# Four bias tables in place of one: replicating a relative-bias table head by head, with pauses, in a two-layer hybrid encoder

## Chip, cores and metric

The kernel runs on 1 core of one Trainium2 chip. The metric is the device time of one execution in microseconds (us), as the median of the runs of one kernel.

## What is computed

The reference is an encoder of two layers on 2048 tokens of width 1024, all in float32. Each layer normalises x, multiplies it by one wide input matrix (1024 x 3584), splits the result among four mixers of 256 channels, gates and joins their outputs and multiplies by an output matrix. The change lies in what mixer D (2-D neighbourhood attention, four heads of 64) needs: a bias that is looked up from a small learned table of each head by the relative row and column of query and key.

```python
def hybrid_layer(x, norm_g, w_in, w_out, ..., na_rpb):
    h = rmsnorm(x, norm_g)
    proj = jnp.einsum("bsd,de->bse", h, w_in)      # split into groups A, B, C, D
    ...
    y_d = neighborhood_attn(d_q, d_k, d_v, na_rpb) * jax.nn.silu(d_z)
    y = jnp.concatenate([y_a, y_b, y_c, y_d], axis=-1)
    return x + jnp.einsum("bse,ed->bsd", y, w_out)

def neighborhood_attn(q, k, v, rpb):               # rpb (4 heads, 15, 31)
    ...
    bias = jnp.take(rpb[:, dr], dc, axis=-1)       # dr, dc: relative row and column
    scores = jnp.where(col_ok[:, None, :], scores + bias[None], NEG_INF)
    p = jax.nn.softmax(...)
```

## The kernel before

**Staging.** Channels stand on the 128 partitions and tokens in four chunks of 512 columns; two chunks at a time are resident (slots s0 and s1). Every float32 operand of the large products is split into a high and a low part, and each product is three matmuls (line 906). A weight tile is loaded in two halves of 256 KB into one of three buffers `wraw` (`load_w`, line 879), split by ScalarE into `whi` (line 218) and by VectorE into `wlo` (line 219), and then used by 12 matmuls of 512 columns for each chunk (`run`, line 894). The matmul helper `mm` is line 135, and VectorE's instructions all stand at line 128.

**Order of the work.** The order is written by generators in Python. After each group of 8 of the large matmuls `run` calls `point()` (line 180), which advances every generator of the lists `evs`, `units` and `bg` by one step; `hold(n)` (line 212) lets n such points pass. There are 864 groups in the kernel: 336 for the input product of a layer, 96 for its output product. In the first half of a layer the first three weight tiles are run for one chunk and then again for the other (3 points a tile, so weights are loaded twice as densely there), and the tiles between are run for both chunks (6 points a tile).

Attention is cut into *units* (line 646): one kind (C or D), chunk, head pair and quarter. A unit begins at most every 5 points (`SPACING`), loads q, holds 7 points and then issues its score matmuls at the next one. A group of four units begins once its `ready` mark and its bias table are `done` (`add_units`, line 785): units of chunk 0 of layer 0 need the table of layer 0, and all others the table of layer 1. The marks come from the tiles of the input product: `("qd", 0, 0)` 8 points after the eighth tile and `("qd", 0, 1)` 8 points after the twelfth tile of the second half. The output product of a chunk needs the attention outputs Y of that chunk, loaded and split by `place_y_steps` (line 343).

On top of this a scheduler of the framework puts each engine's instructions in the order in which they become ready in its own timeline, by priority, so that a transfer without a dependency can be issued long before its place in the program. `tc.keep_in_program_order` pins an instruction behind the one that was traced before it on the same engine. All transfers of the kernel are issued by SyncE (SP), one after the other: a transfer that waits holds up those behind it.

**The bias table.** `bias_steps(l)` (line 792) runs once for each layer: for layer 0 as a background generator as soon as chunk 1 is staged (`early`, line 1126), for layer 1 as a unit after the last units of chunk 0 (line 1078). It copies the 18 KB of the layer's four zero-padded head tables to 128 rows of `rep` in DRAM (line 795, 2256 KB), holds 4 points, and gathers for each head 128 shifted windows of 737 elements into `bm` (line 804, 368.5 KB each; the first three in the `ks` buffers, the last in a `vt` buffer of the attention). Then nine mask pieces `bmk` are loaded (line 809), GpSimd subtracts (line 817) and the result is stored to `bias` (line 821); each of the nine takes 6 points of the program.

Of the kernel before, what the change touches and what calls it, by code (L numbers as in the profile page):

```python
# [18 lines left out]
P = 128  # L19
# [11 lines left out]
RPW = 47  # L31
RPR = 24
# [3 lines left out]
def window(i, j):  # L36
    R, C = DROWS[i][1], DCOLS[j][1]
    return (15, 5, C) if (R, C) == (16, 24) else (R, 4, C)
# [33 lines left out]
def trunk(ctx, tc, xT, w_in, w_out, par, sink, rpb, fg, trig, cmask, dmask, out):  # L72
    nc = tc.nc
    pe, act, dve, pool, sp = nc.tensor, nc.scalar, nc.vector, nc.gpsimd, nc.sync
# [14 lines left out]
    def T(pool_, shape, dt, tag, bufs, name=None):  # L89
        uid[0] += 1  # L90
        return pool_.tile(shape, dt, tag=tag, bufs=bufs, name=f"{name or tag}_{uid[0]}")
# [54 lines left out]
    def dram(name, shape, dt=F32):  # L146
        return dr.tile(shape, dt, name=name)

    LP = []
    for l in range(DEPTH):  # L150
        L = {"par": par_t[l]}
        L["aw"] = L["par"][:, PAW:PAW + 62]
        L["bw"] = L["par"][:, PBW:PBW + 6]
        for nm, w in (("lbh", 2), ("lbq", 2), ("sink", 4), ("nsink", 4)):
            L[nm] = const.tile([P, w], F32, name=f"{nm}{l}")
        L["KD"] = [dram(f"KD{l}_{p}", [2, P, SEQ]) for p in range(2)]
        L["QD"] = [dram(f"QD{l}_{p}", [2, 64, SEQ // P, 2 * P]) for p in range(2)]
        L["KC"] = [dram(f"KC{l}", [2, P, SEQ])]
        L["QC"] = [dram(f"QC{l}_{p}", [2, 64, SEQ // P, 2 * P]) for p in range(2)]
        L["VC"] = dram(f"VC{l}", [P, 2, SEQ // P, P])  # L160
        L["VD"] = [dram(f"VD{l}_{p}", [64, 32, 2 * P]) for p in range(2)]
        L["G"] = [dram(f"G{l}_{e}", [P, SEQ]) for e in range(8)]
        L["Y"] = [dram(f"Y{l}_{e}", [P, 2, SEQ]) for e in range(4)]
        L["X"] = dram(f"X{l}", [DM, SEQ])
        L["rep"] = dram(f"rep{l}", [P, 4 * RPR * RPW])
        L["bias"] = dram(f"bias{l}", [4, P, MTOT])
        LP.append(L)

# [43 lines left out]
    def hold(n):  # L212
        for _ in range(n):
            yield
# [576 lines left out]

    def bias_steps(l):
        L = LP[l]
        W = 4 * RPR * RPW
        tc.keep_in_program_order(sp.dma_start(out=L["rep"], in_=rpb[l:l + 1, :].broadcast_to([P, W])))
        yield from hold(4)
        n = 15 * RPW + 32
        Ms = []
        for h in range(4):
            M = T(ap_, [P, 2 * CH], F32, "ks", KSB, "bm") if h < 3 else T(ap_, [P, 2 * CH], F32, "vt", VTB, "bm")  # L800
            base = L["rep"][0:1, :]
            src = bass.AP(tensor=base.tensor, offset=base.offset + h * RPR * RPW + 7 * RPW + 15,
                          ap=[[16 * W - RPW, 8], [W - 1, 16], [1, n]])
            sp.dma_start(out=M[:, :n], in_=src)
            Ms.append(M[:, :16 * RPW].rearrange("p (r c) -> p r c", c=RPW))
        for (o, sz, i, j) in MOFF.values():
            R, rr, C = window(i, j)
            mk = T(ap_, [P, CH], F32, "pth", PTB, "bmk")
            sp.dma_start(out=mk[:, :sz], in_=dmask[:, o:o + sz])
            r0, c0 = ROW_M0[i], COL_M0[j]  # L810
            mkv = mk[:, :sz].rearrange("p (g r c) -> p g r c", r=rr, c=C)
            yield
            yield
            for p in range(2):
                t = T(ap_, [P, 2, CH], F32, "prob", PRB, "bmo")
                for hh in range(2):
                    pool.tensor_tensor(out=t[:, hh, :sz].rearrange("p (g r c) -> p g r c", r=rr, c=C), in0=mkv,
                                       in1=Ms[2 * p + hh][:, r0:r0 + R, c0:c0 + C].rearrange(
                                           "p (r g) c -> p g r c", r=rr), op=ALU.subtract)
                yield from hold(2)  # L820
                sp.dma_start(out=L["bias"][2 * p:2 * p + 2, :, o:o + sz].rearrange("h q n -> q h n"), in_=t[:, :, :sz])
        done.add(("bias", l))
# [251 lines left out]
    for l in range(DEPTH):  # L1074
        add_units(l, "d", 0, ("qd", l, 0))
        add_units(l, "c", 0, ("qc", l, 0))
        if l == 0:
            waiting.append((lambda: all(("c", 0, 0, 1, j) in done for j in range(4)), deque([lambda: bias_steps(1)])))
        for c in (1, 2, 3):
            add_units(l, "d", c, ("qd", l, 1))  # L1080
            add_units(l, "c", c, ("qc", l, 1))
# [44 lines left out]
    def early():  # L1126
        while (0, 1) not in acts:
            yield
        yield from bias_steps(0)
# [80 lines left out]
```

## Time and profile before

| | |
|---|---|
| median of 3 runs | 2021.67 us (2020.09 to 2022.21) |
| the profiled execution's own time | 2031.42 us |
| its span, first to last instruction | 2029.4 us |
| mean granted TensorE clock | 0.988 of full speed |
| TensorE matmul busy | 1953.2 us (96%), 9600 instructions |
| VectorE busy | 1484.6 us (73%) |
| ScalarE busy | 1042.1 us (51%) |
| GpSimd busy | 147.3 us (7%) |
| DMA | 402.74 MB, mean 198 GB/s |

Times of rows are microseconds from the start of the span unless marked ns. Engines: PE is TensorE (PEld its weight loads), DVE VectorE, ACT ScalarE, POOL GpSimd, SP SyncE; SPq is a transfer's issue on SyncE's queue. Names such as `wraw<-in_w_in_dram` are output and input tiles of an instruction, with buffer numbers left out.

### The profile page before, as it was taken

The page shows a single profiled execution, that of the slowest core. Times are in us where ns is not written, and L with a number is a line of the kernel's source. Part 1 is how long each engine was busy: PE and PEld are TensorE (multiplying, and loading weights), DVE is VectorE, ACT ScalarE, POOL GpSimd, SP SyncE. Part 2 cuts the span into 40 slices and gives each one's busy share as a digit, 9 for nine tenths or more (in the row PEclk, how much of TensorE's full clock was granted, in tenths as well). Part 3 has the DMA queues.
Part 4 walks back from the last instruction along what each step waited for, and adds up shares of the span by engine and source line. Part 5 has one row for each costly group of instructions (what it writes and reads, how often), then busy time and mean ns, then how long its engine had stood idle before and what let it go on. Part 6 is the DMA issues. An engine that isn't in the chain of part 4 may idle for free.

```text
span 2029.4 us, 29478 instructions
## 1 busy us (share of the span) xinstructions
PE 1953.2 (96%) x9600; PEld 1637.2 (81%) x9600; DVE 1484.6 (73%) x3209; ACT 1042.1 (51%) x2219; POOL 147.3 (7%) x138
## 2 busy tenths in 40 slices
PE   6999999989999999999999999999999999999997
PEld 5778888768788887878888888878888788888876
DVE  7434799927995686677465999777896668777865
ACT  5335444423265556567575445644225676777631
POOL 0241000042010020000010000001001001000000
PEclk9999999989999999999999999999999999999998
DMA  6995432588446369887754445876545984777573
GB/s 203 299 350 184 141 104 92 170 257 252 147 141 209 96 217 297 257 249 217 236 175 148 123 151 181 273 228 216 159 153 168 268 247 135 220 231 229 159 237 120
DMA packets 235001, 402.74 MB, mean 198 GB/s; under 512 B 26976, under 2 KB 92128, under 8 KB 234592
## 3 DMA queue, kind: packets, MB, share of 16 engines
q1 hardware_dynamic: 234848, 400.87, 63.9%
q8 instruction: 76, 1.25, 0.3%
q14 instruction: 77, 0.63, 0.1%
HBM read 299.78 MB, written 105.61 MB: 200 GB/s over the span
## 4 chain that ended last, share of the span: by engine, by line
PE 77%; DMA 13%; DVE 7%; issue 1%; ACT 1%; SPq 1%; DVEq 0%; ACTq 0%
PE mm L135 63%; DMA wraw<-in_w_out_dram 4%; PE s L135 4%; PE o L135 4%; PE pt L734 4%; DMA wraw<-in_w_in_dram 2%; DVE wlo L128 1%; DMA rep<-in_rpb_dram 1%; DVE accA L128 1%; DMA s1l<-Y 1%; PE rb L135 1%; DMA VD<-hv 1%; DVE xt L128 1%; DVE s1l L128 1%; PE cs L135 1%
## 5 line engine op out<-in xcount | busy, mean ns | idle before, releaser
L218 ACT CAST whi<-wraw 128x512 fp32r<-128x512 f32 x408 | 252.2, 618 | 447.0 <-PE mm L135 288.3
L135 PE MATMUL mm<-s1h,whi 128*128 128x512 f32 x1152 | 458.2, 398 | 22.9 <-ACT whi L218 14.1
L135 PE MATMUL mm<-s0h,whi 128*128 128x512 f32 x1152 | 453.4, 394 | 6.8 <-ACT whi L218 4.2
L135 PE MATMUL mm<-s1h,wlo 128*128 128x512 f32 x1152 | 457.7, 398 | 1.6 <-DVE wlo L128 1.6
L135 PE MATMUL mm<-s1l,whi 128*128 128x512 f32 x1152 | 457.3, 397 | 0.0
L135 PE MATMUL mm<-s0l,whi 128*128 128x512 f32 x1152 | 453.1, 393 | 1.8 <-DVE s0l L128 1.8
L135 PE MATMUL mm<-s0h,wlo 128*128 128x512 f32 x1152 | 453.7, 394 | 0.9 <-DVE wlo L128 0.9
L128 DVE TENSOR_TENSOR wlo<-wraw,whi 128x512 fp32r<-128x512 f32 x408 | 291.3, 715 | 206.7 <-ACT whi L218 187.2
L128 DVE SCALAR_TENSOR_TENSOR accA<-gA,par,accA 128x1024 f32<-128x1024 f32 (+1 forms) x240 | 310.4, 1312 | 0.7
L135 PEld LDWEIGHTS mm<-s1h,whi 128*128 128x128 f32 x1152 | 219.7, 191 | 70.4 <-ACT whi L218 18.8
L135 PEld LDWEIGHTS mm<-s1h,wlo 128*128 128x128 f32 x1152 | 219.9, 191 | 48.8 <-DVE wlo L128 4.9
L135 PEld LDWEIGHTS mm<-s0h,whi 128*128 128x128 f32 x1152 | 217.3, 189 | 50.9 <-ACT whi L218 6.1
L135 PEld LDWEIGHTS mm<-s1l,whi 128*128 128x128 f32 x1152 | 219.9, 191 | 44.0 <-issue 0.5
L135 PEld LDWEIGHTS mm<-s0l,whi 128*128 128x128 f32 x1152 | 216.9, 188 | 44.9 <-DVE s0l L128 2.5
L135 PEld LDWEIGHTS mm<-s0h,wlo 128*128 128x128 f32 x1152 | 217.0, 188 | 44.0 <-DVE wlo L128 2.2
L707 ACT ACTIVATE prob<-prob,mn 128x384 f32<-128x384 f32 (+4 forms) x256 | 155.6, 608 | 83.3 <-DVE mn L128 82.3
L128 DVE TENSOR_TENSOR pth<-pt,pth 128x512 fp32r<-128x512 f32 (+3 forms) x248 | 138.0, 572 | 31.1 <-ACT pth L218 30.0
L724 ACT ACTIVATE prob<-prob,sm 128x384 f32<-128x384 f32 (+4 forms) x256 | 142.2, 603 | 32.2 <-DVE sm L128 30.3
L218 ACT CAST pth<-pt 128x512 fp32r<-128x512 f32 (+3 forms) x248 | 114.9, 496 | 73.3 <-PE pt L734 42.6
L135 PE MATMUL s<-ks,qs 128*128 128x384 f32 (+4 forms) x512 | 123.5, 345 | 6.6 <-DMA ks<-KD 4.3
L135 PE MATMUL o<-pth,vt 128*128 128x256 f32 (+2 forms) x784 | 127.1, 288 | 2.0 <-DVE pth L128 1.1
L135 PEld LDWEIGHTS o<-pth,vt 128*128 128x128 f32 (+2 forms) x784 | 111.9, 190 | 12.8 <-DVE pth L128 2.9
(122 smaller groups left out, 1995.9 us busy)
## 6 DMA issues: line engine op xcount, KB each, us to landing
wraw<-in_w_in_dram SPq DMA_DIRECT2D x280, 256.0 KB
wraw<-in_w_out_dram SPq DMA_DIRECT2D x128, 256.0 KB
qs<-QD SPq DMA_DIRECT2D x128, 128.0 KB
qs<-QC SPq DMA_DIRECT2D x128, 128.0 KB
G<-g SPq DMA_DIRECT2D x48, 256.0 KB
vt<-VD SPq DMA_DIRECT2D x144, 72.0 KB
xt<-in_xT_dram SPq DMA_DIRECT2D x20, 512.0 KB
KD<-t SPq DMA_DIRECT2D x32, 256.0 KB
```

The lines of the kernel that those rows point to most:

```text
L128: return fn(*a, **kw)
L135: pe.matmul(out=out, lhsT=lhsT, rhs=rhs, start=start, stop=stop)
L218: act.copy(out=hi, in_=src)
L707: act.activation(out=t[:, hh, :n], in_=t[:, hh, :n], func=AF.Exp, bias=mn[:, hh:hh + 1], scale=-1.0, accum_out=sm[:, hh:hh + 1])
L724: act.activation(out=t[:, hh, :n], in_=t[:, hh, :n], func=AF.Copy, scale=sm[:, hh:hh + 1])
L734: pe.transpose(out=tp[:kw, b_, hh, :], in_=t[:, hh, kb * kw:(kb + 1) * kw], identity=ident)
```

## The change

`rep` becomes four DRAM tables, one for each head. `bias_steps` issues four copies of 564 KB, each pinned in program order and each followed by a hold of 3 points. Before each of the four gathers there is a new hold of 2 points, and gather h reads table h, so that it depends on copy h alone. Bytes moved, masks, subtraction and stores are as before. Counted in points, the first gather stands 14 points after the first copy where it stood 4, and the end of the generator 74 points after it where it stood 58.

```diff
-        L["rep"] = dram(f"rep{l}", [P, 4 * RPR * RPW])
+        L["rep"] = [dram(f"rep{l}_{h}", [P, RPR * RPW]) for h in range(4)]
...
     def bias_steps(l):
         L = LP[l]
-        W = 4 * RPR * RPW
-        tc.keep_in_program_order(sp.dma_start(out=L["rep"], in_=rpb[l:l + 1, :].broadcast_to([P, W])))
-        yield from hold(4)
+        W = RPR * RPW
+        for h in range(4):
+            tc.keep_in_program_order(sp.dma_start(out=L["rep"][h],
+                                                  in_=rpb[l:l + 1, h * W:(h + 1) * W].broadcast_to([P, W])))
+            yield from hold(3)
         n = 15 * RPW + 32
         Ms = []
         for h in range(4):
+            yield from hold(2)
             M = T(ap_, [P, 2 * CH], F32, "ks", KSB, "bm") if h < 3 else T(ap_, [P, 2 * CH], F32, "vt", VTB, "bm")
-            base = L["rep"][0:1, :]
-            src = bass.AP(tensor=base.tensor, offset=base.offset + h * RPR * RPW + 7 * RPW + 15,
+            base = L["rep"][h][0:1, :]
+            src = bass.AP(tensor=base.tensor, offset=base.offset + 7 * RPW + 15,
                           ap=[[16 * W - RPW, 8], [W - 1, 16], [1, n]])
             sp.dma_start(out=M[:, :n], in_=src)
```

## Rows read from the trace of the kernel before

**Rows 1.** The page, part 1: busy time and share of the span by engine.
```profile
PE 1953.2 (96%) x9600; PEld 1637.2 (81%) x9600; DVE 1484.6 (73%) x3209; ACT 1042.1 (51%) x2219; POOL 147.3 (7%) x138
```
**Rows 2.** Stretches: length, busy PE, PEld, DVE, ACT, POOL; clock, DMA share, GB/s.
```profile
62.30:66.60 4.30, 0.04 (x2) 0.02 (x1) 0.04 (x1) 0.62 (x1) 0.00 (x0) 1.00 0.95 320
66.60:70.50 3.90, 3.90 (x10) 2.82 (x11) 2.30 (x4) 1.76 (x3) 0.00 (x0) 0.56 0.94 330
...
410.90:415.00 4.10, 0.16 (x1) 0.00 (x0) 0.01 (x1) 1.22 (x2) 0.00 (x0) 1.00 0.84 282
415.00:418.50 3.50, 3.49 (x9) 2.61 (x9) 2.05 (x3) 1.24 (x2) 0.00 (x0) 0.52 0.57 176
...
425.10:429.60 4.50, 0.02 (x1) 0.02 (x1) 0.04 (x1) 0.62 (x1) 4.24 (x6) 0.91 0.71 201
429.60:435.40 5.80, 5.63 (x12) 3.94 (x13) 3.91 (x5) 1.24 (x2) 0.77 (x1) 0.50 0.98 288
435.40:446.40 11.00, 11.00 (x49) 9.11 (x48) 2.30 (x3) 1.76 (x4) 9.20 (x10) 0.99 0.86 293
```
**Rows 3.** ScalarE's timeline: weight splits; in brackets the idle time before and its end.
```profile
65.92 0.62 ACT L218 CAST whi<-wraw 128x512 fp32r<-128x512 f32 x1 [6.97 <-DMA wraw<-in_w_in_dram]
...
414.34 0.62 ACT L218 CAST whi<-wraw 128x512 fp32r<-128x512 f32 x1 [2.64 <-DMA wraw<-in_w_in_dram]
...
428.91 0.62 ACT L218 CAST whi<-wraw 128x512 fp32r<-128x512 f32 x1 [11.96 <-DMA wraw<-in_w_in_dram]
```
**Rows 4.** SP's timeline: when transfers were issued; start, time of the issues, count.
```profile
15.12 1.69 SPq L809 DMA_DIRECT2D bmk<-in_dmask_dram  x2
...
52.70 0.60 SPq L795 DMA_DIRECT2D rep<-in_rpb_dram  x1
...
55.82 0.57 SPq L882 DMA_DIRECT2D wraw<-in_w_in_dram  x1
...
65.22 2.61 SPq L804 DMA_DIRECT2D bm<-rep  x4
...
401.10 0.57 SPq L795 DMA_DIRECT2D rep<-in_rpb_dram  x1
...
402.95 0.68 SPq L882 DMA_DIRECT2D wraw<-in_w_in_dram  x1
...
413.22 2.67 SPq L804 DMA_DIRECT2D bm<-rep  x4
...
416.58 0.34 SPq L882 DMA_DIRECT2D wraw<-in_w_in_dram  x1
```
**Rows 5.** The chain that ended last, transfers on it: issue, time until landing.
```profile
52.70 12.51 DMA rep<-in_rpb_dram
65.22 7.25 DMA bm<-rep
...
91.62 7.30 DMA trig<-in_trig_dram
...
375.01 6.08 DMA wraw<-in_w_in_dram
...
401.10 12.11 DMA rep<-in_rpb_dram
...
416.58 12.23 DMA wraw<-in_w_in_dram
```
**Rows 6.** SP's own waits over the span: total us, times, longest.
```profile
SPq L804 <- DMA rep<-in_rpb_dram: 10.5, 2, 6.3
```
**Rows 7.** Large matmuls alone, from the start to two times (PE's x is their count).
```profile
0.00:180.00 180.00, 141.18 (x588) 111.66 (x588) 8.95 (x13) 24.18 (x42) 0.99 0.79 264
0.00:346.20 346.20, 288.79 (x1201) 225.04 (x1201) 21.96 (x32) 35.05 (x60) 1.00 0.61 197
```
**Rows 8.** Chunk 1 before the output product: last splits of Y, first matmul on them.
```profile
798.94 1.14 ACT L218 CAST s1h<-s1l 128x512 fp32r<-128x512 f32 x2
...
827.68 0.39 PE L135 MATMUL mm<-s1h,whi 128*128 128x512 f32 x1
```

## Prediction, made before the change was run

> **What bounds the kernel now.** I read the page first: TensorE is busy for 96% of the span, VectorE for 73%, everything else less [rows 1]. So time is gained only where TensorE stands still or runs slowly, and lost only where it is made to. Next I listed TensorE's timeline for stretches without a matmul. Outside the first 30 us and the very end, the three longest are 62.3 to 66.6, 410.9 to 415.0 and 425.1 to 429.6 us, and all three lie just behind the copies of the bias table [rows 2, 4]. After each pause the clock is low as well: the granted clock is 0.50 to 0.56 in the next 4 to 6 us, close to the lower of the two levels, 1.2 of 2.4 GHz [rows 2].
>
> ScalarE's timeline says what TensorE waited for: a weight half to split, and that half was late by DMA, by 6.97, 2.64 and 11.96 us of ScalarE's idle time [rows 3]. SP's timeline says why. Behind the first copy (52.70) a weight load was issued at 55.82, and ScalarE got it only at 65.92, when the copy was also through [rows 3 to 5]. Behind the second copy (401.10) a load went out at 402.95 and its split began at 414.34, one microsecond after the copy landed at 413.21 [rows 3 to 5]. Then SP itself was closed: the four gathers wait for the copy, in two waits of 10.5 us together, the longer 6.3 us [rows 6]; with their own issues (2.67 us) they held the next weight load back until 416.58, and that load, behind four gathers in the transfer queue, needed 12.23 us where another needed 6.08 [rows 4, 5].
>
> So the present cost is: one large copy that blocks the transfer queue (A at 62.3, B at 410.9), and one wait plus a burst of gathers that blocks SP and then the queue (C at 425.1).
>
> **What these three cost.** In an undisturbed stretch TensorE does 49 matmuls in 11.00 us, 0.225 us each [rows 2]. A: 62.3 to 70.5 is 8.2 us for 2 + 10 matmuls, worth 2.7 us, so 5.5 us are lost. B: 410.9 to 418.5 is 7.6 us for 1 + 9, worth 2.2, so 5.4 lost. C: 425.1 to 435.4 is 10.3 us for 1 + 12, worth 2.9, so 7.4 lost. Sum 18.3 us, clock included, all on TensorE's own path.
>
> **The change, part by part.**
>
> *Four copies, 3 points apart.* A point is 8 matmuls, at least 8 x 0.225 = 1.8 us, so copies start some 5.4 us apart. The whole copy took 12.51 and 12.11 us [rows 5]; a quarter of the bytes holds the queue back by about a quarter of that, 3.1 us, before the next piece comes. In A the weight half was split from 65.92; with three quarters of the copy (9.4 us) not in front of it, it would be there before 62.3. Even if only the 6.08 us of another weight load held, it would be there at 61.9, and a split of 0.62 us follows: at worst some 0.5 us remain. In B the load of 402.95 would be there by 409.0 instead of 414.3, before TensorE runs dry at 410.9. I take 0.5 us of rest for each. The landing of one 564 KB piece is not in the trace: from below 3.1 us (the quarter), from above 7.30 us (a 512 KB load in the busy stretch of layer 0) [rows 5]. I take some 4 to 5 us; the upper end is a rival below. The six more issues cost SP 6 x 0.6 = 3.6 us over the kernel [rows 4], beside TensorE's work.
>
> *A gather that follows its own table.* By the program's order the first gather comes 14 points, at least 25 us, after its copy, and the last 11 points, 20 us, after its own. Both exceed the 12.5 us of the whole copy, so in that order SP never waits: the 10.5 us go. The scheduler can put a gather earlier (it put mask loads at 15.12, before the copy that their piece follows in the program [rows 4]); then SP waits for a small piece instead of the large one, for at most the landing minus what the scheduler assumed.
>
> *Holds between the gathers.* 2 points, 3.6 us, stand between gathers that each move 368.5 KB; the four together landed in 7.25 us [rows 5], so about 1.8 us each. A weight load then has one gather ahead, not four. I leave 1.0 us of C. Together: 18.3 less 0.5, 0.5 and 1.0 is 16.3 us gained.
>
> *A later table.* Each table is finished 16 points later in the program. What hides that? In layer 0 nothing at first: the first unit's scores come after 588/8 = 73.5 points [rows 7], 8 points after the unit begins, so it began at 65.5, and the mark `("qd", 0, 0)` stood ready at 18 + 5 x 6 + 8 = 56. The table was last, so all 16 units of chunk 0 move by 16 points. Their last scores come at 1201/8 = 150.1 points [rows 7], 5.1 points a unit. Add 13 points to the unit's end: 163, where the second table begins. Before, it ended at 163 + 58 = 221, while its users also wait for `("qd", 0, 1)` at 168 + 72 + 8 = 248. So 27 points are spare there. After: 163 + 16 + 74 = 253, only 5 points past the mark. The units of chunks 1 to 3 of layer 0 thus move by about 5 points, 9 to 13 us. In layer 1 the next mark comes much later and takes it up.
>
> Who is hurt? The output product of chunk 1 needs Y: it was split by 800.1, and the first matmul on it came at 827.68 [rows 8], 27.6 us of cover against 9 to 13 us. Moving units does not add work on TensorE, and VectorE, idle in most of the stretch after 407 us [rows 2], has room for those of chunk 0 there. The cost is between -2 us (work in that room) and +5 us (chunk 1 a little late); I take +1.3 us.
>
> **Sum.** 16.3 - 1.3 = 15.0 us. Against the profiled execution: 2031.4 - 15.0 = 2016.4 us (its span 2029.4 lies within 2.0 us of it). That execution is 9.75 us above the median of the runs, and the stalls should be as long in both, so I subtract the same from the median: 2021.7 - 15.0 = 2006.7 us.
>
> **Rivals.**
>
> *Four waits for one (slower).* If the scheduler puts each gather right behind its copy, SP waits four times a layer. Four pieces at 7.30 us are 29.2 us in which SP is mostly closed to weight loads, where one copy took 12.1 to 12.5: 17 us more a layer. For it: gathers can move forward, and the queue was 0.94 to 0.95 busy around A [rows 2]. Against it: the copies are pinned at 5.4 us and more apart, and weight loads get through between. It decides once a piece lands later than about 5.4 us and its gather already stands at SP's head. If half of the added 2 x 17 us comes through to TensorE on top of today's 18.3, it is 2021.7 + 17 = 2039 us. Chance 0.08.
>
> This is also what a rule would expect: the Trainium skill, "DMA: Bandwidth & Descriptors", section "Rules for kernel authors", wants at least 1 MiB in a DMA for full bandwidth and small transfers joined; the change cuts 2256 KB into pieces of 564 KB. By that rule alone the sum would be this rival's 2039 us, not 2006.7. The trace speaks for the other side: there it is the large copy's length, not its efficiency, that TensorE pays for [rows 3, 5].
>
> *Attention runs late (slower).* If the spare 27 points are not there, chunk 1 moves by up to 32 points, about 73 us at 2.3 us a point with units between; less the cover of 27.6 us [rows 8] and the gain of 15, that is 2021.7 + 30 = 2052 us. It needs more than 12 points of delay; I count 5. Chance 0.05.
>
> *Nothing changes.* The queue is busy anyway (0.71 to 0.98 in and after the three pauses [rows 2]), and other loads take the room: 2021.7 us. Against it: each pause ends within a few us of a landing copy or gather. Chance 0.09.
>
> *Half.* The copies no longer block, but the gathers still come as a burst, so C stays and A leaves a rest: 2021.7 - 9 = 2012.7 us. Chance 0.14.
>
> **How the numbers follow.** The forecast has the remaining 0.64, from 2000 us (all 18.3 and 2 us of relief on VectorE) to about 2011. Runs of this kernel spread over 2.1 us, so about 0.2%, 4 us, is what a measurement can tell from no change. The range 1999 to 2019 holds the forecast and the half case, 0.78, and a small part of the unchanged case. Faster by more than 0.2% (below 2017.6): forecast and most of half, 0.76. Slower (above 2025.7): the two slower rivals and a little of the unchanged case, 0.14. Within: 0.10.
>
> **What would show it.** In the changed profile: eight copies of about 0.6 us issue time each on SP, 5 us or more apart; SP's waits for `rep` well below 10.5 us; no pause of TensorE over 1.5 us within 40 us of a copy or gather, and no half clock there; first unit's scores near 89 points; chunk 1's Y split still before its matmuls. The prediction is wrong if the pauses stay, move to the gathers, or come back before the output product.

## The result, and the profile after

**The changed kernel is slower: 2042.84 us (median of 4 runs, 2039.62 to 2043.90) against 2021.94 us (4 runs, 2020.09 to 2024.54) for the kernel before; the ratio on record is 1.0076 with a 95% interval of 1.0053 to 1.0100.** The two medians alone would give 1.0103; against the medians of 2025.34 to 2027.12 us that the kernel before had in the longer sets below, 2042.84 us is a ratio of 1.0078 to 1.0086. The text goes by the ratios on record. The forecast was 2006.7 us. The profiled execution took 2043.9 us, its span is 2041.3.

Part 1 of the changed kernel's page has the same work on every engine; TensorE's 1960.6 us stand against 1953.2 [rows 1]:

```profile
PE 1960.6 (96%) x9600; PEld 1646.3 (81%) x9600; DVE 1488.9 (73%) x3209; ACT 1044.8 (51%) x2219; POOL 149.0 (7%) x138
```

At the places of the three pauses there is none any more. The same stretches as in [rows 2], in the changed kernel, and two later ones (length, busy PE, PEld, DVE, ACT, POOL; clock, DMA share, GB/s):

```profile
62.30:66.60 4.30, 4.30 (x20) 3.37 (x19) 1.66 (x3) 2.07 (x4) 0.00 (x0) 1.00 1.05 362
...
98.80:104.10 5.30, 0.11 (x2) 0.04 (x1) 0.00 (x0) 0.66 (x2) 3.09 (x5) 0.92 1.07 384
104.10:110.00 5.90, 5.90 (x16) 4.74 (x17) 1.58 (x3) 2.39 (x4) 3.77 (x4) 0.50 0.99 275
410.90:415.00 4.10, 4.10 (x22) 3.36 (x21) 2.39 (x5) 2.41 (x5) 0.00 (x0) 1.00 0.57 189
...
425.10:429.60 4.50, 4.50 (x21) 3.73 (x20) 0.92 (x2) 1.23 (x2) 0.00 (x0) 1.00 0.73 249
...
459.10:465.60 6.50, 0.12 (x2) 0.10 (x1) 6.36 (x10) 0.00 (x0) 4.99 (x6) 0.70 0.92 313
465.60:471.00 5.40, 5.40 (x22) 4.76 (x23) 4.04 (x7) 3.68 (x6) 2.91 (x4) 0.73 0.97 275
```

TensorE is busy throughout where the pauses A, B and C were, at full clock. But there are two new holes, one some 35 us behind the place of A and one as far behind that of C, each with a low clock in or after it. TensorE's timeline of the changed kernel names what ended them (in brackets the idle time and its end):

```profile
104.06 0.79 PE L135 MATMUL mm<-s1h,whi 128*128 128x512 f32 x1 [5.19 <-ACT t L372]
...
465.53 2.04 PE L135 MATMUL rb<-ident,rl 128*128 128x128 f32 x8 [6.38 <-DVE rl L128]
```

SP's timeline has the copies and gathers, here three copies and the first gather of layer 0 and the last copy and three gathers of layer 1 (start, time of the issues, count; against [rows 4]):

```profile
53.66 0.59 SPq L796 DMA_DIRECT2D rep<-in_rpb_dram  x1
...
56.73 0.90 SPq L796 DMA_DIRECT2D rep<-in_rpb_dram  x1
...
62.94 0.77 SPq L796 DMA_DIRECT2D rep<-in_rpb_dram  x1
...
64.69 0.70 SPq L807 DMA_DIRECT2D bm<-rep  x1
...
427.56 0.50 SPq L796 DMA_DIRECT2D rep<-in_rpb_dram  x1
428.15 1.98 SPq L807 DMA_DIRECT2D bm<-rep  x3
```

and its waits for the copies fell from 10.5 us [rows 6] to:

```profile
SPq L807 <- DMA rep<-in_rpb_dram: 2.8, 2, 1.7
```

The attention of chunk 0 moved as forecast. The large matmuls alone, counted up to the first unit's scores, are now 728, so 91.0 points, where they were 588, 73.5 points [rows 7]:

```profile
0.00:214.98 214.98, 175.20 (x728) 139.21 (x728) 12.34 (x18) 28.31 (x48) 0.98 0.75 243
```

**Where the time went.** I compared the times at which two kernels begin their n-th large matmul. Such a difference still contains the small matmuls of the attention that TensorE did before: all six kernels with a late first table (the changed one, e2, e4, e9, e12 and e13 below) have 46 of them fewer behind them at point 164 than e0, and have gained 5.9 us on it since point 48. At the points of the table, other than 352, 384 and 544, the counts differ by 8 at most. The reference here is a second profile of the kernel before, e0 below (span 2018.9 us); point = 8 large matmuls; us later (+) or earlier (-) than e0:

| kernel | 32 | 48 | 192 | 208 | 352 | 384 | 544 | 592 | 704 | 848 |
|---|---|---|---|---|---|---|---|---|---|---|
| before, the first profile | -2.5 | -0.8 | +3.3 | +2.1 | +7.3 | +7.0 | +7.0 | +10.4 | +10.8 | +10.4 |
| **changed** | -5.3 | +2.5 | -8.0 | +0.1 | +0.9 | +3.0 | +1.1 | +14.8 | +15.8 | +22.9 |
| e1 four copies, no holds | -1.0 | +1.7 | +7.6 | +6.5 | +7.2 | +5.0 | +4.9 | +7.7 | +7.5 | +2.7 |
| e2 holds alone | -1.7 | -2.0 | -12.4 | -12.3 | -3.6 | -0.6 | -2.6 | +13.8 | +14.5 | +16.0 |
| e3 changed, on time | -7.4 | -0.2 | +0.3 | -0.9 | +0.7 | 0.0 | -0.1 | +0.6 | +0.7 | +7.1 |
| e6 mark 6 points later | -1.8 | -2.1 | -2.3 | -3.5 | -4.4 | +7.7 | +5.8 | +15.0 | +15.7 | +28.6 |
| e7 mark 12 points later | -0.9 | -1.0 | +1.4 | +0.2 | -5.8 | +8.2 | +8.6 | +17.5 | +16.6 | +18.5 |
| e8 before, two loads by GpSimd | -2.7 | -0.8 | +0.3 | +0.7 | +0.4 | -3.3 | -3.4 | -5.0 | -6.1 | -5.8 |
| e9 changed, two loads by GpSimd | -7.9 | -0.6 | -11.0 | -3.1 | -1.9 | -0.6 | -2.6 | 0.0 | +1.0 | +2.9 |
| e11 e6, two loads by GpSimd | -0.9 | -1.2 | +2.8 | +3.2 | +0.3 | +9.2 | +7.3 | +9.1 | +9.9 | +8.2 |
| e12 changed, xo loads by GpSimd | -7.9 | -1.5 | -12.0 | -10.4 | +0.4 | +3.4 | +1.5 | +4.6 | +5.5 | +14.3 |
| e13 changed, loads of G by GpSimd | -8.0 | -1.9 | -12.5 | -4.3 | -4.3 | -0.2 | -2.2 | +8.7 | +9.4 | +15.7 |

Two executions of one kernel differ by up to 10 us in such a row (the first line), so only what repeats over several kernels counts. Three things do. The gain at A is there at point 32 and gone at 48. Behind the place of B and C the changed kernel is 8.0 us ahead at 192 and level at 208. And between 544 and 592 it loses 13.7 us, as e2 does (16.4) and, less, e6 and e7 (9.2 and 8.9), where the first profile of the kernel before, e1 and e3 lose 3.4 at most. This stretch lies in points 552 to 600, the output product of chunks 2 and 3 of layer 0, where neither a table nor a copy is near. e6 and e7 lose more in another place, 12.1 and 14.0 us between 352 and 384, the output product of chunks 0 and 1, in which they have 28 and 26 more small matmuls; the changed kernel loses 2.1 us there.

### The profile page after: what moved, and what is told of

It is laid out like the page before. It is cut to its first block, busy times and chain, and to the rows that moved or that the text cites. A ratio compares the mean times of both kernels' runs of the same rounds, so it can differ in the third digit from the quotient of the medians.

```text
span 2041.3 us, 29465 instructions
## 1 busy us (share of the span) xinstructions
PE 1960.6 (96%) x9600; PEld 1646.3 (81%) x9600; DVE 1488.9 (73%) x3209; ACT 1044.8 (51%) x2219; POOL 149.0 (7%) x138
## 2 busy tenths in 40 slices
DMA packets 235865, 402.74 MB, mean 197 GB/s; under 512 B 27072, under 2 KB 92224, under 8 KB 235712
## 5 line engine op out<-in xcount | busy, mean ns | idle before, releaser
L135 PE MATMUL mm<-s1h,whi 128*128 128x512 f32 x1152 | 456.3, 396 | 15.8 <-ACT t L372 7.6
L128 DVE SCALAR_TENSOR_TENSOR accA<-gA,par,accA 128x1024 f32<-128x1024 f32 (+1 forms) x240 | 306.2, 1293 | 0.7
L135 PEld LDWEIGHTS o<-pth,vt 128*128 128x128 f32 (+2 forms) x784 | 112.5, 192 | 12.5 <-ACT es L710 1.7
```

Source lines behind the costliest of these rows:

```text
L128: return fn(*a, **kw)
L135: pe.matmul(out=out, lhsT=lhsT, rhs=rhs, start=start, stop=stop)
```

## The experiments

Theories, as the expectations name them. **1**: the tables cost by being late; 1a: only because the table of layer 1 ends past the mark `("qd", 0, 1)`, 1b: each late table costs for itself. **2**: the pieces of the copy and the waits for them cost. **3**: the new program merely got an unlucky order from the scheduler. Then, for the place of the loss, **S**: SP is closed to weight loads there; **W**: the units' own work collides with the output product's; **D**: issuing from GpSimd has a price of its own.

| run | kernel | median us | ratio to before, 95% interval |
|---|---|---|---|
| e0 | before, unchanged | 2025.57 | 0.9993 (0.9974 to 1.0012) |
| e1 | four copies, no holds | 2025.75 | 0.9989 (0.9977 to 1.0002) |
| e2 | holds alone | 2041.67 | 1.0069 (1.0050 to 1.0089) |
| e3 | changed, tables on time | 2020.78 | 0.9978 (0.9958 to 0.9998) |
| e4 | changed, table 0 alone late | 2022.26 | 0.9975 (0.9955 to 0.9996) |
| e5 | changed, table 1 alone late | 2022.36 | 0.9986 (0.9961 to 1.0010) |
| e6 | before, mark 6 points later | 2048.82 | 1.0105 (1.0066 to 1.0145) |
| e7 | before, mark 12 points later | 2038.75 | 1.0067 (1.0045 to 1.0089) |
| e8 | before, both loads by GpSimd | 2018.88 | 0.9972 (0.9956 to 0.9989) |
| e9 | changed, both loads by GpSimd | 2023.04 | 0.9987 (0.9971 to 1.0004) |
| e10 | e3, both loads by GpSimd | 2013.83 | 0.9934 (0.9911 to 0.9957) |
| e11 | e6, both loads by GpSimd | 2030.76 | 1.0024 (1.0003 to 1.0045) |
| e12 | changed, xo loads by GpSimd | 2027.65 | 1.0013 (0.9990 to 1.0035) |
| e13 | changed, loads of G by GpSimd | 2035.26 | 1.0048 (1.0032 to 1.0064) |
| e14 | changed, subtraction on VectorE (6 runs) | 2040.45 | 1.0076 (1.0050 to 1.0101) |
| e15 | e10, subtraction on VectorE | 2017.12 | 0.9968 (0.9951 to 0.9985) |

The kernel before ran beside each set, with medians from 2025.34 to 2027.12 us; ratios are compared.

**Parts of the change (e0 to e3).** e0 is the kernel before.

> The kernel before, unchanged, for a second profiled execution beside that of the changed kernel and for the scatter of the timing. All theories: 2020 to 2025 us, ratio 1.000 within 0.002. The three pauses of TensorE behind the two copies (4.3, 4.1 and 4.5 us) should come again; the open question is whether the profile's span (2029.4) was 8 us above the timed runs by a stretch that can be named.

e1 has the four tables and copies one behind the other, the old hold of 4 and no holds between gathers:

```diff
-            yield from hold(3)
+        yield from hold(4)
...
-            yield from hold(2)
```

> Four tables and four copies as in the changed kernel, but the copies one after the other, then one hold of 4 points, and no hold before the gathers: the generator ends at 58 points as before. Theory 1 (the table that is done 16 points later costs the time): no loss behind the copies' stretch, the first unit's scores at 73 to 75 points, and 2010 to 2024 us. Theory 2 (the pieces and the waits of the single gathers cost it): 2035 to 2045 us. Theory 3 (any change of the order shifts the scheduler's whole result by chance): anywhere from 2005 to 2045, with losses at other places than in the changed kernel.

e2 keeps the one table and one copy, and takes the holds alone: 12 points behind the copy and 2 ahead of each gather, so that the program's points are the changed kernel's:

```diff
-        yield from hold(4)
+        yield from hold(12)
...
         for h in range(4):
+            yield from hold(2)
```

> One table and one copy as before, then a hold of 12 points and 2 points before each gather: the generator ends at 74 points as in the changed kernel. Theory 1: the loss of the changed kernel is here too, 2038 to 2060 us, and pause A behind the first copy stays (about 4 us). Theory 2: 2015 to 2024 us, since nothing is in pieces. Theory 3: anywhere from 2005 to 2045.

e3 is the changed kernel, with the 16 points saved elsewhere in the same generator: eight of the nine mask pieces skip their two points, so that the table ends at 58 points as before.

```diff
-        for (o, sz, i, j) in MOFF.values():
+        for im, (o, sz, i, j) in enumerate(MOFF.values()):
...
-            yield
-            yield
+            if im == 0:
+                yield from hold(2)
```

> The changed kernel with 16 points taken from the mask steps behind the gathers (no hold of 2 points in eight of nine masks), so that the table is done 58 points after the first copy as before, while copies and gathers keep their pauses. Theory 1: 2003 to 2018 us, first unit's scores at 73 to 75 points. Theory 2: 2035 to 2045 us. Theory 3: anywhere from 2005 to 2045.

Cutting the copy costs nothing and gains nothing (0.9989). The holds alone, without any cut, cost what the whole change costs (1.0069 against 1.0076). The whole change with tables on time costs nothing, and is 0.22% faster. So it is theory 1, and 2 falls.

The profiles also say which pause went by what. In e0 they came again, behind points 16, 180 and 184: A 5.68, B 4.12, C only 1.44 us. Copies one behind the other (e1) remove none: 5.30, 8.41 and 2.81 us. Pieces with holds remove A, and in its place comes the wait for `t` at point 32 (e3 4.53 us, the changed kernel 5.19). B and C are another matter. e3, whose pieces are issued at points 165 to 175, about where the one copy stood (174.6), still has waits of 2.00 and 3.17 us for a weight at points 183 and 184, and is not ahead at 192. e2, whose one uncut copy comes 10 points later (184.6), has no wait over 0.8 us from 396 to 480 us, and is 12.4 us ahead at 192. So what took B and C out of the changed kernel is the later place of its second table (its copies lie at 179 to 187), not the pieces.

A rule bears on e1: the Trainium skill, "DMA: Bandwidth & Descriptors", section "Rules for kernel authors", asks for at least 1 MiB in a DMA; here 564 KB pieces in place of 2256 KB made no difference, so the measurement decides for this kernel.

**Which table, and is it the mark (e4 to e7)?** e4 and e5 are e3 with the two points skipped for one layer only:

```diff
-            if im == 0:
+            if im == 0 or l == 0:
```

(e5: `l == 1`.)

> As the run whose table is on time, but the table of layer 0 alone is 16 points late (its masks keep all their holds). By the count the table of layer 1 then ends at 237 points, 11 before the mark at 248: the units of chunk 0 of layer 0 move, the later ones do not. Theory 1a (only what goes past that mark costs, because it moves the units of chunks 1 to 3 and of layer 1's chunk 0): 2015 to 2028 us, ratio 0.995 to 1.002, no loss between the points 544 and 592. Theory 1b (each late table costs for itself): half of the changed kernel's loss, ratio 1.003 to 1.007.

> The same with the table of layer 1 alone 16 points late: it ends at 163 + 74 = 237 points, again 11 before the mark. Theory 1a: ratio 0.995 to 1.002 and no loss between the points 544 and 592. Theory 1b: ratio 1.003 to 1.007.

e6 and e7 leave the tables as before and move only the mark, by 6 and by 12 points:

```diff
-                yield from hold(8)
+                yield from hold(14 if ks == [("qd", 0, 1)] else 8)
```

> The kernel before with its single table and copy, and only the mark that lets the units of chunk 1 of layer 0 begin set 6 points later (14 for 8), about what the late table does in the changed kernel. Theory 1a: the loss of the changed kernel without any change of the tables: ratio 1.004 to 1.010, with some 15 us lost between the points 544 and 592, as there. Theory 1b and any theory that needs the late table itself: ratio 0.998 to 1.002.

> The same with the mark 12 points later. Theory 1a as a steady dose: about twice the loss of the run with 6 points, ratio 1.010 to 1.018. Theory 1a as a collision (the units of layer 1's chunk 0 fall on another stretch of the output product): the loss is at the same points but not proportional. Theory 3 (the scheduler's order by chance): no relation to the 6 points, and losses at other places.

Each table alone is harmless: with table 0 late and table 1's generator short, or the other way round, table 1 ends at 237 points, ahead of the mark. Only both together pass it. And the mark alone, with nothing of the change in the kernel, makes the loss: 1.0105 and 1.0067. That is theory 1a; 1b falls. The mark itself stands at 251 in the program's count: to the 240 points of the tiles come two that pass while the kernel waits for its second chunk, and `hold(8)` ends on the ninth. The table's 253 is thus 2 points late, not 5, and the traces show it: counted in large matmuls, the third, fifth and seventh unit of layer 0's chunk 1 begin their scores at 265.5, 277.0 and 287.0 points in both profiles of the kernel before, at 267.0, 279.0 and 289.0 in the changed kernel and e2, at 273.0, 283.0 and 293.0 in e6, at 279.0, 289.0 and 299.0 in e7. So 2, 6 and 12 points cost 0.76 (e2: 0.69), 1.05 and 0.67%: it is not a price per point but a collision at some place, and by the table of times not at the same place in all. Of e6's loss 9.2 us arise at 544 to 592, where its expectation had some 15. Theory 3 is not excluded by any one run, but the changed kernel and e0 to e7, nine kernels that differ in their code, fall into two classes by whether units wait past the mark's old place.

The traces show the shift. The stores of Y end the groups of units, and their place, in points, hardly varies. Layer 1's first four groups, those of its chunk 0, stand at

| kernels | points of the four stores of Y |
|---|---|
| before (two profiles), e1, e3, e4, e5 | 530, 554 to 555, 568, 579 to 581 |
| changed, e2 | 534, 559, 572, 582 |
| e6 | 538, 562, 576, 586 |
| e7 | 539, 566, 579, 589 |
| all of them, the next group | 707 |

So the 2 points are passed on to layer 1's chunk 0 and are 2 to 5 points at its stores; its units follow on those of layer 0 without a wait for a mark, and the next mark does take the delay up, but only ahead of 707. In between lies the output product of points 552 to 600.

**What collides there (e8 to e11).** Points 576 to 592 alone, all of TensorE (columns as above). In e0:

```profile
1320.40:1358.60 38.20, 38.11 (x196) 31.82 (x195) 29.59 (x67) 17.07 (x31) 0.00 (x0) 1.00 0.73 230
```

and in the changed kernel:

```profile
1326.00:1373.40 47.40, 43.78 (x208) 36.82 (x207) 33.14 (x76) 19.60 (x36) 0.00 (x0) 0.89 0.71 219
```

Twelve more small matmuls fall into this stretch, but it is 9.2 us longer, with a granted clock of 0.89 and 3.6 us without a matmul. ScalarE waits there for weights, and what stands behind the late split waits with it. In the changed kernel, ScalarE's timeline:

```profile
1334.50 0.62 ACT L218 CAST whi<-wraw 128x512 fp32r<-128x512 f32 x1 [6.38 <-DMA wraw<-in_w_out_dram]
1335.02 0.63 ACT L861 ACTIVATE sq<-xo 128x512 f32<-128x512 f32 x1
```

and TensorE's:

```profile
1335.70 0.59 PE L135 MATMUL cs<-ones,sq 128*128 128x1 f32 x2 [2.58 <-ACT sq L861]
...
1338.61 1.62 PE L135 MATMUL o<-pth,vt 128*128 128x256 f32 x6 [1.04 <-DVE oy L128]
```

These two waits are the 3.6 us; the second ends with VectorE's work for a unit, not with a weight.

Why is the weight late? The DMA engines are not fuller (0.71 against 0.73). But SP, which issues the weight loads, is closed for longer. Its own waits between 1318 and 1375 us (total, times, longest), in e0:

```profile
SPq L843 <- DMA X<-xo: 13.2, 5, 4.3
...
SPq L718 <- DMA Y<-ag: 3.0, 1, 3.0
```

in the changed kernel:

```profile
SPq L846 <- DMA X<-xo: 21.1, 6, 4.2
SPq L718 <- DMA Y<-ag: 5.7, 2, 2.9
```

These are the same times, not the same points. Over points 552 to 600 the two waits are 27.6 and 4.8 us in e0, 36.5 and 7.5 us in the changed kernel. The late weight above is the load of 1328.03, the first weight load behind such a wait; SP's timeline in the changed kernel (SP stood still from 1323.98 to 1327.12):

```profile
1323.56 0.42 SPq L662 DMA_DIRECT2D prob<-bias  x1
1327.12 0.33 SPq L846 DMA_DIRECT2D xo<-in_xT_dram  x1
1327.51 0.43 SPq L273 DMA_DIRECT2D xt<-X  x1
1328.03 0.42 SPq L885 DMA_DIRECT2D wraw<-in_w_out_dram  x1
```

The two kinds of wait are those of a load for a store that must free its buffer: the load of `xo` (the residual, line 846) for the store of an earlier `xo`, the load of G (line 718) for the store of Y. In the output product weights are used by 12 matmuls for one chunk, which take 2.7 us (12 x 0.225 [rows 2]), so a wait of 3 to 4 us ahead of a load can be felt. To test it, both kinds of loads go to GpSimd's queue, which is idle there; nothing else in the program changes.

```diff
-            sp.dma_start(out=g, in_=L["G"][...])
+            pool.dma_start(out=g, in_=L["G"][...])
...
             x = T(gp, [P, CH + 3], F32, "gB", GB, "xo")[:, :CH]
-        sp.dma_start(out=x, in_=src[dt * P:(dt + 1) * P, cs(c)])
+            pool.dma_start(out=x, in_=src[dt * P:(dt + 1) * P, cs(c)])
+            return x
```

> Edit: the kernel before, with two kinds of transfers issued by GpSimd instead of SP: the xo loads of the output product (they wait for a slot that an earlier X store frees) and the loads of G behind each attention group (they wait for a Y store). It is the control for the other three of this set. Theory S (a late shift costs through SP being closed to weight loads in the output product by these two waits): SP's waits for X<-xo and Y<-ag (29 us and some of the window 1318 to 1375 had 16 us in the kernel before) vanish; the kernel is 0 to 10 us faster than before, 2015 to 2027 us. Theory W (the units' own work, on VectorE and ScalarE, collides with the output product's): no change, 2024 to 2029. Theory D (issuing from GpSimd costs something of its own): slower by over 5 us.

> Edit: the changed kernel with the same two kinds of transfers issued by GpSimd. Theory S: the loss is gone, within 5 us of the control e8 (ratio to it 0.995 to 1.003), and points 576 to 592 take below 43 us (47.1 in the changed kernel, 38 in the kernel before). Theory W: the loss stays, 12 to 25 us above e8, and points 576 to 592 take 45 us or more.

> Edit: the on-time version (e3) with the same two kinds of transfers issued by GpSimd. Theory S: e8 less 0 to 6 us. Theory W: the same, so this one does not tell them apart; it is the candidate for a version faster than both kernels (below 2020 us).

> Edit: the kernel before with the mark (qd, 0, 1) 6 points later (e6) and the same two kinds of transfers issued by GpSimd. Theory S: the 1.05% that the mark cost is gone, ratio to e8 below 1.003. Theory W: it stays, 12 to 25 us above e8. If one of e9 and e11 keeps its loss and the other does not, both waits and work have a part.

The same points 576 to 592 in e9, with the same 208 matmuls as the changed kernel:

```profile
1319.20:1358.60 39.40, 39.40 (x208) 33.10 (x208) 31.28 (x70) 18.91 (x34) 3.22 (x6) 1.00 0.71 222
```

39.4 us, busy throughout, at full clock: 8.0 us less for the same matmuls. The score matmuls of layer 1's chunk 0 stand at the same points as in the changed kernel, to 0.1, and their work is all there, so W can have at most the rest: from 544 to 592 e9 loses 4.2 us to e8, where the changed kernel lost 13.7 to e0, and the whole of points 552 to 600 takes 110.3 us in e9 as in e8, 122.5 in the changed kernel, 112.6 in e0. (The last two stores of Y of e9 are back at 569 and 580 points: a store's place also depends on when SP is free.) The moved loads also travel in a queue of their own, 16.78 MB of 402.74, so the weights could have become faster in transit instead of being issued earlier. They were issued earlier: the eight weight loads that e9 issues from 1315 to 1339 us lie 8.0 to 10.1 us ahead of their splits, the six of the changed kernel from 1318 to 1337 us 4.1 to 9.6 us, that of 1328.03 6.5 us, with ScalarE waiting for it. In time, the changed kernel against the kernel before is 1.0076; with both loads moved in both it is 0.9987 / 0.9972 = 1.0015, which the two intervals (each 0.17% wide to a side) do not tell from nothing. Of the 0.76%, some 0.6 is SP. For the moved mark, theory S fell short of its number: 1.0024 / 0.9972 = 1.0052 is left of 1.0105. In e11 most of the rest arises at 352 to 384, in the output product of chunks 0 and 1, which takes 89.6 us against 76.9 in e8, with two waits of TensorE for `whi`, 5.31 and 1.34 us; at 552 to 600 it is 114.2 against 110.3 (e6 against e0: 121.9 and 112.6). A delay of 6 points also collides in the first place; the 0 to 2 points that the changed kernel has there do not. What e11's weights wait for was not followed further.

A rule speaks against e8: the Trainium skill, "SBUF — State Buffer", section "SBUF: two separate sides", warns that transfers issued by GpSimd stall while VectorE runs an operation that holds the port the two share, and advises SP or ScalarE. By that rule e8 could be slower. Here VectorE is busy for 73% of the span [rows 1], how much of it with such operations no run shows, and e8 is 0.28% faster, so such stalls, if there are any, cost less than the open SP brings.

**Which of the two waits (e12, e13)?** One kind of loads each:

> Edit: the changed kernel with only the xo loads issued by GpSimd; the loads of G stay on SP. If the xo wait (21.1 us of SP in the window 1318 to 1375) is what closes SP: as e9, 2019 to 2027 us, points 552 to 600 in 109 to 113 us (122.3 in the changed kernel). If it is the G wait (5.7 us there, 39.4 us over the span): 2035 to 2045 us and about 120 us there. If both have a part: 2028 to 2034.

> Edit: the changed kernel with only the loads of G issued by GpSimd; the xo loads stay on SP. The other half of e12: if the xo wait closes SP, 2035 to 2043 us and points 552 to 600 in 118 to 123 us; if it is the G wait, 2019 to 2027 us; if both, between.

Moving the `xo` loads alone takes the ratio from 1.0076 to 1.0013, moving those of G alone to 1.0048, both together to 0.9987: 0.63, 0.28 and 0.89%. Over the whole time both have a part, and the `xo` wait has the larger, as its 21.1 us against 5.7 let expect. In the stretch itself it is the `xo` wait alone: points 552 to 600 take 110.3 us in e12, as in e9, and 120.2 in e13, as the first of the two forecasts had it. Where the loads of G earn their part was not followed.

**Where the lead behind B and C went (e14, e15).** In the hole at 465.53 TensorE waits for `rl`, the end of a chain of short VectorE instructions. Their durations in the changed kernel, VectorE's timeline:

```profile
455.75 0.16 DVE L128 TENSOR_TENSOR rn<-rn,rn 128x4 f32<-128x4 f32 x1
...
456.07 1.18 DVE L128 TENSOR_TENSOR rn<-rn,rn 128x4 f32<-128x4 f32 x1
...
458.45 1.10 DVE L128 SCALAR_TENSOR_TENSOR rn<-rl 128x4 f32<-128x4 f32 x1
```

One instruction takes 0.16 or 1.18 us, beside eight subtractions that run back to back on GpSimd, its timeline:

```profile
456.04 8.04 POOL L820 TENSOR_TENSOR bmo<-bmk,bm 128x512 f32<-128x512 f32 x8 [0.43 <-POOL bmo L820]
```

e14 and e15 put the subtraction on VectorE, in the changed kernel and in e10:

```diff
-                    pool.tensor_tensor(out=t[:, hh, :sz]..., op=ALU.subtract)
+                    dve.tensor_tensor(out=t[:, hh, :sz]..., op=ALU.subtract)
```

> Edit: the changed kernel with the 72 subtractions of the tables on VectorE in place of GpSimd; nothing else. If GpSimd beside VectorE is what slows the short instructions of the chain to rl: those of 128x4 elements between 449 and 465 us take 0.15 to 0.2 us (0.68 to 1.12 in the changed kernel), TensorE's wait of 6.38 us for rl there is below 2 us, and the time is 3 to 6 us shorter, since the 72 subtractions (some 0.4 us each on VectorE, an estimate from its 128x512 instructions) lie beside other work; 2037 to 2041 us. If the chain is merely late: the wait stays at 4 us or more and the time is unchanged or a few us longer.

> Edit: e10 (tables on time, both kinds of loads on GpSimd's queue) with the subtractions on VectorE. If GpSimd slows VectorE generally: 2 to 6 us faster than e10, so 2008 to 2012 us. If only that one chain suffers, which in e10 showed no such wait: 2012 to 2016 us, no difference. If VectorE is short of time around 70 to 100 us or 440 to 480 us: slower, 2016 to 2020.

e14's own trace, of an execution of 2794.31 us, is not used, so its two signs in the profile stay open. In e15 all 26 instructions of the two chains that run side by side there take 0.15 to 0.17 us. VectorE's timeline, the two kinds shown above:

```profile
458.53 0.16 DVE L128 TENSOR_TENSOR rn<-rn,rn 128x4 f32<-128x4 f32 x1
...
458.92 0.16 DVE L128 SCALAR_TENSOR_TENSOR rn<-rl 128x4 f32<-128x4 f32 x1
```

So GpSimd does slow them. But it is not what the time hangs on: e14 is where the changed kernel is (1.0076 both), and e15 is, if anything, slower than e10 (0.9968 against 0.9934). My reading of the lead behind B and C as lost to this chain falls. e12 shows what stands behind it: there the chain costs TensorE only 1.22 us, the kernel is 10.4 us ahead of e0 at point 208, and 4.0 at 224. ScalarE's timeline of e12 in between:

```profile
496.50 0.62 ACT L218 CAST whi<-wraw 128x512 fp32r<-128x512 f32 x1 [9.57 <-DMA wraw<-in_w_in_dram]
```

Whichever wait is removed, another comes some 40 us later. From 400 to 520 us the DMA engines have a share of 0.80 at 254 GB/s in e0, of 0.82 at 257 in the changed kernel and of 0.80 at 258 in e12, and TensorE is busy for 111.55, 111.25 and 113.00 of the 120 us. That the transfers of this stretch set its length is what these numbers suggest; no run here took transfers out of it, so it stays argued.

**A faster version.** e10, the change with its tables on time and both kinds of loads on GpSimd's queue, is faster than both kernels: 2013.83 us, 0.9934 (0.9911 to 0.9957).

## Why the prediction was wrong

*What bounds the kernel* held: A, B and C are where TensorE stood still, and they stand behind the copies and gathers in both profiles of the kernel before. *What the three pauses cost* held for A and B; C, sized from one execution in which it was 4.50 us long, was 1.44 us in e0.

*Four copies, a gather that follows its own table, holds between the gathers*: SP's wait fell to 2.8 us as said, and the first scores came at 91.0 points (89 were named). The rest of the mechanism is shown for A alone. The copies did not start 5 us apart but 3.1, 6.2 and 3.9 us in layer 0, the first gather came 11.0 us behind its copy and not 25, and the gathers of layer 1 came as a burst of three (428.15), without harm. That B and C are gone is due to the table's later place, as e2 and e3 show. And by the prediction's own sign, no pause over 1.5 us and no half clock within 40 us of a copy or gather, it failed: the holes at 98.8 and 459.1 us lie in that reach.

*"18.3 less 0.5, 0.5 and 1.0 is 16.3 us gained" failed*: it took the length of a pause for its price. Of the gain at A nothing is left at point 48, of the lead behind B and C nothing at 208, since the next wait (`t` at 104.06, `rl` at 465.53) ends where the old one would have let TensorE arrive. With tables on time the whole change is worth 0.22% (e3), or 0.9934 / 0.9972, so about 0.38%, with SP open (e10 against e8): 4 to 8 us, not 16. The rival "nothing changes" described this part.

*"In layer 1 the next mark comes much later and takes it up" failed, and it decided the sign.* The table's end at 253 was counted right; the mark stands at 251 and not at 248, so the delay was 2 points where 5 were named, and the stores of Y show 2 to 5. The next mark does take it up, ahead of point 707. But the units of layer 1's chunk 0 follow directly on those of layer 0, ahead of that mark, and carry the delay into the output product of chunks 2 and 3.

*The cover of 27.6 us* [rows 8] was counted for the wrong thing. Y of chunk 1 was not late: its last split began at 798.13 us, against 798.94 [rows 8]. The term was sized at -2 to +5 us, taken as 1.3; the stretch from 544 to 592 cost 13.7 us against e0. It is not the wait for a late result, but units at another place of a stretch in which SP has no time to spare.

*The rival "attention runs late"* had the right kind of cause and the right sign, the wrong place (Y of chunk 1) and the wrong threshold: it asked for more than 12 points, and 2 were enough. *"Four waits for one"*, the rival of the same sign on the pieces, did not occur: SP waited for the copies twice, not eight times, and e1 has no loss.

The bound of 0.2% for what can be told from no change came from three runs that spread over 2.1 us; the four sets of 23 to 29 runs of the kernel before spread over 14 to 19 us.

What stays open: from point 704 to 848 the changed kernel loses a further 7.1 us to e0, e9 only 1.7 us to e8, e2 1.5 us to e0. In e0 and e3 the same stretch differs by 6.4 us, so this may be nothing but the scatter of single executions.

## What to carry to other kernels

Where the order of work is fixed by counted steps, follow a delay to the last unit that it moves, across layers, before calling it taken up; and where it ends among other work, ask which queue issues that work's loads, not only whether its inputs are there. On an engine that issues all transfers in order, a load that waits for a store to free its buffer blocks every load behind it: such loads belong on another queue, which here was worth 0.28% to the kernel before and made the late units harmless. A stall that is removed is worth at most what the next wait leaves. And a pause that is gone was not removed by the edit that was meant to remove it until a kernel with that edit alone shows so: here one uncut copy at a later place had no B and C either.

## What the runs showed of the hardware

Short VectorE instructions of 128x4 elements, 0.15 to 0.17 us by themselves, took up to 1.18 us beside GpSimd's subtractions, seven times as long, and returned to 0.15 to 0.17 us once those ran on VectorE (e15). I had not expected this to reach instructions so small: it turns a chain of 13 into a wait. That the time did not improve without it (e14, e15) is the other half of that finding.
